# State-space scan over chunks of eight steps, with the first raw activations read back ahead of the residual

## The chip, the cores and the metric

One core of a Trainium2 chip runs the whole program. The metric is device time in microseconds (us), the median over several runs; the profile is of one execution. TensorE multiplies matrices, VectorE, ScalarE and GpSimd (POOL in the profile) work on elements, SyncE (SP) does nothing but issue DMAs.

## What is computed

A two-block transformer over 256 tokens of width 1024, in fp32. The first block runs sliding-window attention and a state-space layer side by side, adds both to the input, and then a retrieval layer (8 heads pick 16 of 16384 single-neuron experts each). A second block has two attention layers. The part that matters here is the state-space layer, over 272 positions (16 meta tokens and 256 tokens): 32 groups of 16 channels, each of which drives 64 complex states.

```python
def s5_ssm(u, a_re, a_im, log_dt, b_re, b_im, c_re, c_im, d, glu_w, glu_b):
    ...
    _, _, s_r, s_i = lax.associative_scan(_complex_linear_combine, (a_r, a_i, bu_r, bu_i), axis=1)
    y = (jnp.einsum('blgn,gpn->blgp', s_r, c_re.astype(jnp.float32))
         - jnp.einsum('blgn,gpn->blgp', s_i, c_im.astype(jnp.float32))
         + d.astype(jnp.float32).reshape(SSM_GROUPS, SSM_CH) * uf)
    z = jax.nn.gelu(y.reshape(B, L, SSM_WIDTH), approximate=False)
    z = z * jax.nn.sigmoid(z @ glu_w.astype(jnp.float32) + glu_b.astype(jnp.float32))
```

Before it, a fixed complex factor abar and a map bbar are made of the parameters, and bu is bbar times the input of a step: s(t) = abar s(t-1) + bu(t), y(t) = Re(c s(t)) + d u(t).

## The kernel before

`body` (line 1583) runs four stages: `first_half` (line 176: the first attention and the state-space layer), `peer` (line 725: the retrieval layer), `even` and `odd` (the second block). A framework records all instructions, works out their dependencies and puts each engine's instructions in an order by the times that it expects; at run time each engine, and SP's queue of DMAs, goes through its own list in order. `c.after(b, a)` fixes that b is put behind a.

Weights come in half tiles of 128x1024 fp32 through `Feed` (line 63): SP loads them (line 88) into five buffers, ScalarE rounds each to H (line 100), and VectorE or GpSimd subtracts to get the rest Lo (line 102); a product of matrices is then three passes, H by H, H by Lo and Lo by H (`mm3`, lines 1643 to 1645). SP can load into a buffer only when Lo of its last contents is done.

In `first_half` the input is normalised and turned (`turn(k)`, lines 227 to 233, of which hH and hL, lines 232 and 233, are the two halves), and u is projected from it into four accumulators (`up`). Then a background of three generators, `kv`, `q` and `attention`, is interleaved by hand with the state-space layer: `f.run` (line 439) draws a step from `ssm_scan` and lets the background spend the number of ns that the step yields. The output projection of the attention half (`out_part`, added to h at line 356) ends the background; the state-space half's own `out_part` ends the stage.

The state-space layer goes by 8 groups of two pairs of channel groups, step by step in time. `ssm_setup` (line 449) makes tables tabc and tabs of the cosine and sine of the state's angle for 137 steps, by doubling (lines 547 to 559). `ssm_scan` (line 563) maps u to the states on TensorE (line 590), turns them by the tables so that the recurrence becomes real (`turn`, lines 597 on GpSimd and 599 on VectorE, sums at lines 628 and 629), scans in two halves of 136 steps on VectorE (line 637, joined at lines 641 to 645), turns back, and maps the states to the outputs on TensorE (line 614). The d term, Gelu, the GLU's matmuls (line 658) and `ssm_glu` follow. At line 262 ScalarE's queue fills wscr, 8 MB in DRAM, with zeros.

In `peer`, a first expert phase multiplies the normed input with 16384 columns and stores the raw activations of two blocks at a time in DRAM (ascr<-ga, line 792). Meanwhile GpSimd scatters the picked weights into wscr, one indirect DMA a slot (`scatter`, line 997, DMA at line 1002), and then fetches them (line 804). The second expert phase reads the raw activations back (`back`, line 818, DMA at line 820), multiplies them by the weights (line 845), splits them (lines 847 and 848) and multiplies with the second expert matrix (line 835). Before its first matmul `refill` (line 1697) allocates c.x, which takes the place of xH, and loads the residual (line 1702) and the parameters of the second block (line 1704). In the recorded code the first two reads stand before `refill`, but their order on SP is the framework's.

Of the kernel before, what the change touches and what calls it, by code (L numbers as in the profile page):

```python
# [19 lines left out]
FT = mybir.dt.float32  # L20
# [31 lines left out]
NPKA = _cols(PKA, [("are", 16), ("aim", 16), ("ldt", 16), ("n1g", 8), ("pow", 8)])  # L52
NPK1 = _cols(PK1, [("bre", 256), ("bim", 256), ("cre", 256), ("cim", 256), ("d", 4), ("glub", 4), ("ag", 4), ("sg", 4),
# [119 lines left out]
HL = L // 2  # L173


def first_half(c):
# [4 lines left out]
    with ExitStack() as ctx:  # L181
# [26 lines left out]
        tab = ssm_setup(c, one, inp, P1)  # L208
        S5 = next(tab)
# [5 lines left out]
        uT = one.tile([128, 4, L], FT, name="uT")  # L215
        nc.scalar.activation(uT.rearrange("p a b -> p (a b)")[:16, :D], mt, AF.Square, accum_out=ss[:16, 2:3])
# [6 lines left out]
        hH = inp.tile([128, 8, L], FR, name="hH")  # L223
        hL = inp.tile([128, 8, L], FR, name="hL")
# [14 lines left out]
        next(tab, None)  # L239
        for q in range(4):  # L240
            H, Lo = c.feed.take()
            for k2 in range(2):
                k = 2 * q + k2
                for ct in range(4):
                    s = slice(k2 * 512 + ct * 128, k2 * 512 + (ct + 1) * 128)
                    c.mm3(up[ct][:, :L], H[:, s], Lo[:, s], hH[:, k], hL[:, k], k == 0, k == 7)
                if k + 3 < 8:
                    turn(k + 3)
                if k + 3 == 7:
                    for _ in range(4):  # L250
                        next(tab, None)
        uH = one.tile([128, 4, L], FR, name="uH")
        uL = one.tile([128, 4, L], FR, name="uL")
        for ct in range(4):
            nc.scalar.copy(uH[:, ct], up[ct][:, :L])
            c.usplit = V.tensor_sub(uL[:, ct], up[ct][:, :L], uH[:, ct].bitcast(FT))
            nc.scalar.copy(uT[:, ct], up[ct][:, :L])
        for _ in tab:
            pass
        S5[-1]()  # L260
# [176 lines left out]
        zT = one.tile([128, 4, T], FT, name="zT")  # L437
        f.spend(8000)
        f.run(ssm_scan(c, f, one, P1, uH, uL, uT, S5, zT, lambda: glu, res))
        work = ctx.enter_context(tc.tile_pool(name="b1g", bufs=1, side="right", reuse_waits="tile"))  # L440
        zH, zL, zr = ssm_glu(c, work, P1, zT, res["glu"])
# [4 lines left out]
def ssm_setup(c, one, tmp, P1):  # L446

    nc, tc = c.nc, c.tc
    V, G = nc.vector, nc.gpsimd
    small = lambda n, w=16: one.tile([128, w], FT, name=n)  # L450

    dt, ar, th, mag = small("dt"), small("ar"), small("th"), small("mag")
    nc.scalar.activation(dt, P1("ldt"), AF.Exp)
    V.tensor_tensor(th, P1("aim"), dt, op=OP.mult)
    V.tensor_tensor(ar, P1("are"), dt, op=OP.mult)
    nc.scalar.activation(mag, ar, AF.Exp)

    flat = lambda t: t.rearrange("p n j -> p (n j)")
    ang, kk, s2 = (tmp.tile([128, 8, 16], FT, name="pw%d" % i) for i in range(3))
    s1, pc = (one.tile([128, 8, 16], FT, name="pw%d" % i) for i in range(3, 5))  # L460
    V.tensor_tensor(ang, th[:, None, :].to_broadcast([128, 8, 16]), P1("pow")[:, :, None].to_broadcast([128, 8, 16]), op=OP.mult)
    ang, kk, s1, s2, pcf = (flat(t) for t in (ang, kk, s1, s2, pc))
    V.tensor_scalar(kk, ang, 1.0 / (2 * math.pi), MAGIC_ROUND, op0=OP.mult, op1=OP.add)
    V.tensor_scalar(kk, kk, MAGIC_ROUND, None, op0=OP.subtract)
    V.scalar_tensor_tensor(ang, kk, -TWO_PI_HI, ang, op0=OP.mult, op1=OP.add)
    V.scalar_tensor_tensor(ang, kk, -TWO_PI_LO, ang, op0=OP.mult, op1=OP.add)
    V.tensor_scalar(ang, ang, 3.1415925, -3.1415925, op0=OP.min, op1=OP.max)
    nc.scalar.activation(s1, ang, AF.Sin)
    nc.scalar.activation(s2, ang, AF.Sin, scale=0.5)
    tabc = one.tile([128, 16, HL + 1], FT, name="tabc")  # L470
    tabs = one.tile([128, 16, HL + 1], FT, name="tabs")
    bT = [one.tile([128, 2, 4, 128], FR, name="bT%d" % i) for i in range(2)]
    cd = [one.tile([128, 16, 2, 16], FT, name="cd%d" % i) for i in range(3)]
    bd = [tmp.tile([128, 16, 2, 16], FT, name="bd%d" % i) for i in range(2)]
    for t in bd + cd:
        G.memset(t, 0.0)
    V.memset(tabc[:, :, 0:1], 1.0)
    V.memset(tabs[:, :, 0:1], 0.0)
    V.tensor_tensor(s2, s2, s2, op=OP.mult)
    V.tensor_scalar(pcf, s2, -2.0, 1.0, op0=OP.mult, op1=OP.add)  # L480
    ps = s1.rearrange("p (n j) -> p n j", n=8)
    C1, S1 = pc[:, 0], ps[:, 0]
    yield tabc, tabs, mag, bT, cd, lambda: maps_T()


    nr, ni, den, t0, t1, cr, ci = (small("c%d" % i) for i in range(7))
    c.after(V.tensor_tensor(nr, mag, C1, op=OP.mult), c.normed)
    V.tensor_scalar(nr, nr, -1.0, None, op0=OP.add)
    c.after(V.tensor_tensor(ni, mag, S1, op=OP.mult), c.normed)
    V.tensor_tensor(den, P1("are"), P1("are"), op=OP.mult)  # L490
    V.tensor_tensor(t0, P1("aim"), P1("aim"), op=OP.mult)
    V.tensor_tensor(den, den, t0, op=OP.add)
    V.reciprocal(den, den)
    V.tensor_tensor(t0, nr, P1("are"), op=OP.mult)
    V.tensor_tensor(t1, ni, P1("aim"), op=OP.mult)
    V.tensor_tensor(cr, t0, t1, op=OP.add)
    V.tensor_tensor(cr, cr, den, op=OP.mult)
    V.tensor_tensor(t0, ni, P1("are"), op=OP.mult)
    V.tensor_tensor(t1, nr, P1("aim"), op=OP.mult)
    V.tensor_tensor(ci, t0, t1, op=OP.subtract)  # L500
    V.tensor_tensor(ci, ci, den, op=OP.mult)
    yield

    def maps():

        bre, bim = (P1(n).rearrange("p (j q) -> p j q", j=16) for n in ("bre", "bim"))
        m = [tmp.tile([128, 16, 16], FT, name="m%d" % i) for i in range(4)]
        crb, cib = cr[:, :, None].to_broadcast([128, 16, 16]), ci[:, :, None].to_broadcast([128, 16, 16])
        G.tensor_tensor(m[0], bre, crb, op=OP.mult)
        G.tensor_tensor(m[1], bim, cib, op=OP.mult)  # L510
        G.tensor_tensor(m[2], bim, crb, op=OP.mult)
        G.tensor_tensor(m[3], bre, cib, op=OP.mult)
        for g in range(2):
            s = slice(g * 64, g * 64 + 64)
            V.tensor_tensor(bd[0][s, :, g], m[0][s], m[1][s], op=OP.subtract)
            V.tensor_tensor(bd[1][s, :, g], m[2][s], m[3][s], op=OP.add)

    def maps_T():
        cre, cim = (P1(n).rearrange("p (j q) -> p j q", j=16) for n in ("cre", "cim"))
        for z in range(2):  # L520
            p = c.psum("m")
            for i in range(4):
                nc.tensor.transpose(p[:, i * 128:(i + 1) * 128], bd[z][:, 4 * i:4 * i + 4], c.ident)
# [1307 lines left out]
```

## Time and profile before

| | us |
|---|---|
| median of 3 runs | 1405.28 (1401.46, 1405.28, 1407.55) |
| the profiled execution | 1401.81, of which the span is 1400.0 |
| TensorE busy | 1299.6 (93% of the span) |
| VectorE busy | 991.6 (71%) |
| ScalarE busy | 655.1 (47%) |
| GpSimd busy | 527.2 (38%) |
| granted TensorE clock, mean | 0.95 |

The span is the time from the first to the last instruction of the profiled execution. Busy times of engines overlap. A matmul in fp32 leaves two records in the trace, one of fp32r or a transpose leaves one; records of TensorE overlap in its pipeline, so its pace is read from the starts of neighbours or from a row of several. PEclk is the clock that TensorE was granted, as a share of 2.4 GHz.

### The profile page before, as it was taken

What the parts mean: (1) busy time and instruction counts of PE and PEld (TensorE: products, weight loads), DVE (VectorE), ACT (ScalarE), POOL (GpSimd) and SP (SyncE); (2) the same over time, 40 slices, a digit from 0 to 9 for tenths busy, and PEclk for the clock granted to TensorE, in tenths of its full rate; (3) what the DMA queues carried; (4) which work ended last, traced back from release to release, by engine and by line L of the source; (5) the groups of instructions that cost most, each with busy time, mean ns of one, the idle gap of its engine ahead of it and who ended that gap; (6) DMA issues with size and microseconds to landing.
All of it is one profiled execution on the core that took longest, in us unless ns stands there. A gap on an engine that the chain in (4) does not pass through costs nothing.

```text
span 1400.0 us, 21202 instructions
## 1 busy us (share of the span) xinstructions
PE 1299.6 (93%) x7744; PEld 1107.8 (79%) x7744; DVE 991.6 (71%) x2229; ACT 655.1 (47%) x1138; POOL 527.2 (38%) x282
## 2 busy tenths in 40 slices
PE   5677888999999999999799999999998989979998
PEld 4554568999999999999678788888866768766777
DVE  8898957888988766664688855555557765585734
ACT  5323335545445445444444445444454545533552
POOL 4664642188787878600000000000024327441243
PEclk9865898999999999999899999999999999997999
DMA  6820036588888777896899966655664335551231
GB/s 222 287 61 31 16 100 217 163 226 222 224 226 228 190 205 203 256 371 216 281 308 314 308 195 188 188 190 187 193 212 151 90 106 166 198 157 55 82 106 60
DMA packets 103912, 259.01 MB, mean 185 GB/s; under 512 B 27120, under 2 KB 35696, under 8 KB 102528
## 3 DMA queue, kind: packets, MB, share of 16 engines
q1 hardware_dynamic: 65728, 224.04, 49.6%
q10 hardware_dynamic: 17472, 25.17, 5.1%
q0 software_dynamic: 20608, 8.46, 5.0%
q8 instruction: 60, 0.98, 0.3%
q14 instruction: 44, 0.36, 0.1%
HBM read 230.04 MB, written 27.33 MB: 184 GB/s over the span
## 4 chain that ended last, share of the span: by engine, by line
PE 71%; DVE 19%; DMA 5%; issue 3%; POOL 1%; ACT 1%; SPq 0%; DVEq 0%; POOLq 0%; ACTq 0%
PE ps L835 18%; PE ps L1643 10%; PE ps L1644 10%; PE ps L1645 10%; PE pr L1643 4%; PE pr L1645 4%; PE pr L1644 4%; DMA ga<-ascr 4%; DVE Lo L102 3%; PE m L1235 2%; PE ps L1043 2%; PE o L1280 1%; DVE sg L637 1%; DVE rs L1660 1%; POOL pr L597 1%
## 5 line engine op out<-in xcount | busy, mean ns | idle before, releaser
L101 ACT CAST H<-w 128x1024 fp32r<-128x1024 f32 (+1 forms) x370 | 386.5, 1046 | 511.5 <-PE ps L835 182.3
L102 DVE TENSOR_TENSOR Lo<-w,H 128x1024 fp32r<-128x1024 f32 x290 | 364.3, 1257 | 165.9 <-ACT H L101 165.7
L102 POOL TENSOR_TENSOR Lo<-w,H 128x1024 fp32r<-128x1024 f32 (+1 forms) x80 | 193.8, 2427 | 718.8 <-ACT H L101 704.8
L1643 PE MATMUL ps<-xH,H 128*128 128x256 f32 x1024 | 290.8, 284 | 0.0
L835 PE MATMUL ps<-H,a 128*128 128x512 f32 x1024 | 281.3, 396 | 8.0 <-ACT a L847 7.6
L1644 PE MATMUL ps<-xL,H 128*128 128x256 f32 x1024 | 287.8, 281 | 0.0
L1645 PE MATMUL ps<-xH,Lo 128*128 128x256 f32 x1024 | 287.6, 281 | 0.0
L1002 POOL DMA_INDIRECT wscr<-sent x128 | 243.5, 1903 | 72.5 <-issue 37.8
L835 PEld LDWEIGHTS ps<-H,a 128*128 128x128 f32 x1024 | 193.6, 189 | 54.0 <-ACT a L847 7.8
L1643 PEld LDWEIGHTS ps<-xH,H 128*128 128x128 f32 x1024 | 193.1, 189 | 0.0
L1644 PEld LDWEIGHTS ps<-xL,H 128*128 128x128 f32 x1024 | 193.1, 189 | 0.0
L1645 PEld LDWEIGHTS ps<-xH,Lo 128*128 128x128 f32 x1024 | 192.9, 188 | 0.0
L835 PE MATMUL ps<-Lo,a 128*128 128x512 f32 x512 | 161.7, 397 | 0.6 <-DVE Lo L102 0.6
L835 PEld LDWEIGHTS ps<-Lo,a 128*128 128x128 f32 x512 | 96.8, 189 | 24.3 <-DVE Lo L102 1.8
L845 DVE TENSOR_TENSOR act<-ga,act 128x256 f32<-128x256 f32 x128 | 47.3, 420 | 26.8 <-DMA ga<-ascr 26.5
L1643 PE MATMUL pr<-H,exH 128*128 128x512 f32 x128 | 54.5, 427 | 0.9 <-ACT exH L1083 0.9
L847 ACT CAST a<-act 128x256 fp32r<-128x256 f32 x128 | 51.4, 402 | 6.8 <-DVE act L845 6.8
L1643 PE MATMUL pr<-H,oxH 128*128 128x512 f32 (+1 forms) x128 | 52.8, 415 | 1.1 <-ACT oxH L1083 1.1
L848 DVE TENSOR_TENSOR a<-act,a 128x256 fp32r<-128x256 f32 x128 | 53.5, 419 | 0.0
L1644 PE MATMUL pr<-Lo,exH 128*128 128x512 f32 x128 | 53.0, 414 | 0.0
L1645 PE MATMUL pr<-H,oxL 128*128 128x512 f32 (+1 forms) x128 | 52.6, 411 | 0.0
L1030 DVE TENSOR_TENSOR o<-cstt,sel 128x512 f32<-128x512 f32 x32 | 22.1, 692 | 43.0 <-PE ps L1043 43.0
(471 smaller groups left out, 2164.4 us busy)
## 6 DMA issues: line engine op xcount, KB each, us to landing
w<-in_ut SPq DMA_DIRECT2D x128, 512.0 KB
w<-in_pv SPq DMA_DIRECT2D x128, 512.0 KB
ascr<-ga ACTq DMA_DIRECT2D x64, 256.0 KB
ga<-ascr SPq DMA_DIRECT2D x64, 256.0 KB
w<-in_we SPq DMA_DIRECT2D x32, 512.0 KB
w<-in_wod SPq DMA_DIRECT2D x28, 512.0 KB
wscr<-zero ACTq DMA_DIRECT2D x4, 2048.0 KB
w<-in_wqy SPq DMA_DIRECT2D x16, 512.0 KB
```

The costliest lines, as they stand in the source:

```text
L101: self.last = self.nc.scalar.copy(H, self.loaded[u])
L102: eng.tensor_sub(Lo, self.loaded[u], H.bitcast(FT))
L835: nc.tensor.matmul(acc[2 * th + n], a[:, s], b[:, n * 512:(n + 1) * 512], start=first and e == 0, stop=last and e == 2)
L845: V.tensor_tensor(src, ga[:, blk % 2], src, op=OP.mult)
L847: copied = nc.scalar.copy(aH, src)
L848: V.tensor_sub(aL, src, aH.bitcast(FT))
L1002: ins = c.nc.gpsimd.indirect_dma_start(out=c.wscr.rearrange("i b (t o) -> (i b t) o", o=1), out_offset=bass.IndirectOffsetOnAxis(ap=t.bitc ...
L1043: nc.tensor.matmul(p[:, a * 128:(a + 1) * 128], o1[:, a], o2[:, a], start=True, stop=True)
L1235: nc.tensor.matmul(sp[:, :off + nk], q(h)[:, ts], k(h)[:, :off + nk], start=True, stop=True)
L1643: nc.tensor.matmul(o, ah, bh, start=first, stop=False)
L1644: nc.tensor.matmul(o, ah, bl, start=False, stop=False)
L1645: nc.tensor.matmul(o, al, bh, start=False, stop=last)
```

## The change

Instead of a step, the state-space layer now goes by a chunk of 8 steps: 272 positions are 34 chunks. Of each chunk, a matrix W maps its 8x16 inputs to its contribution to the state; a scan over 34 chunks carries the state (one table R of 34 angles); a matrix T maps the 8x16 inputs to the 8x16 outputs inside the chunk (from the impulse response K, which holds d too), and a matrix G maps the state at the chunk's start to its outputs. All four maps are fp32 matmuls. To have a chunk's 8x16 inputs on 128 partitions, u goes through DRAM (udr) and comes back as U in 8 DMAs; K goes through DRAM (kdr) and comes back as T in 16; the outputs z go through DRAM (zdr) in 16 DMAs and come back in 4. All of these are on SP's queue. GpSimd's rotations, the split copies uH and uL and the copy uT go.

```diff
+        if q == 0:
+            ssm.coefficients()
+        ssm.enter(up)
+        ssm.maps()
...
+    def coefficients(self):
...
+        shape = [128, 16, SJ, 16]
+        cut = lambda t: t[:, :16 * SJ * 16].rearrange("p (j m q) -> p j m q", j=16, m=SJ)
+        self.W = [self.temp("W", z) for z in range(2)]
+        t = [self.temp("tw", 2 + z) for z in range(2)]
+        self.product(cut(self.W[0]), cut(self.W[1]), [A[:, z, :, :SJ, None].to_broadcast(shape) for z in range(2)],
+                     [bb[z][:, :, None, :].to_broadcast(shape) for z in range(2)], [cut(x) for x in t])
+    def enter(self, up):
...
+        for ct in range(4):
+            nc.scalar.copy(uP[:, ct].rearrange("p j c -> p c j"), up[ct][:, :L].rearrange("p (c j) -> p c j", j=SJ))
+            nc.sync.dma_start(c.udr[ct * 128:(ct + 1) * 128], uP[:, ct])
+        src = c.udr.rearrange("(g q) j c -> q j g c", q=16)
+        for j in range(SJ):
+            m = SJ - 1 - j
+            nc.sync.dma_start(U[16 * m:16 * m + 16], src[:, j])
+    def response(self):
...
+        nc.sync.dma_start(c.kdr.rearrange("(a p) n -> p a n", p=128), K.rearrange("p a m q -> p a (m q)"))
+        self.T = [one.tile([128, 16, 128], FT, tag="WT", name="T", bufs=2) for z in range(2)]
+        src = c.kdr.rearrange("(g q) n -> q g n", q=16)
+        for h in range(2):
+            for j in range(SJ):
+                m = SJ - 1 - j
+                nc.sync.dma_start(self.T[h][16 * m:16 * m + 16], src[:, 16 * h:16 * h + 16, 16 * m:16 * m + 128])
+    def run(self, glu, out):
...
+                for j in range(j0, j0 + n):
+                    nc.tensor.matmul(p[:, (j - j0) * 2 * SC:(j - j0 + 1) * 2 * SC], self.WT[z][:, j],
+                                     self.U[:, 2 * j:2 * j + 2].rearrange("p g c -> p (g c)"), start=True, stop=True)
...
+        for z in range(2):
+            V.tensor_tensor_scan(flat(sc[:, z]), flat(self.mags), flat(m1[:, z]), 0.0, op0=OP.mult, op1=OP.add)
+        yield 2000
+        self.response()
...
+            if ct % 2:
+                h = slice(8 * ct - 8, 8 * ct + 8)
+                for i in range(SJ):
+                    nc.sync.dma_start(dst[:, i, h], zc[16 * i:16 * i + 16, h])
+                for k in (ct - 1, ct):
+                    nc.sync.dma_start(self.zT[:, k], c.zdr[k * 128:(k + 1) * 128].rearrange("p i c -> p (i c)"))
```

`maps` transposes W (32 transposes into the slots WT, which T takes over later) and makes R by doubling, six levels of six operations; `outputs` makes G, six operations of 128x2304. In `run` the outputs of four channel tiles take 8 matmuls by T (32 columns) and 8 by G (64 columns) each.

The second part fixes the order in which the second expert phase begins: pk2, and then the residual, are put behind the read-back of the second pair of blocks. The third makes scatters wait for the scatters of the head before, and the fetch of wscr for the last ones.

```diff
-            nc.sync.dma_start(ga, c.ascr[blk // AB][:, blk % AB:blk % AB + 2])
+            backs.append(nc.sync.dma_start(ga, c.ascr[blk // AB][:, blk % AB:blk % AB + 2]))
...
-        refill()
+        refill(backs[1])
...
-            nc.sync.dma_start(c.x, hscr)
-            nc.sync.dma_start(pk2, A["pk2"])
+            for m in (nc.sync.dma_start(pk2, A["pk2"]), nc.sync.dma_start(c.x, hscr)):
+                after(m, behind)
...
-                    nc.gpsimd.dma_start(act[:, b, 128:], c.wscr[:, b])
+                    pk.wait(nc.gpsimd.dma_start(act[:, b, 128:], c.wscr[:, b]).ins, pk.last)
...
+        self.wait(ins, self.before)
```

## Rows read from the trace of the kernel before

**Rows 1.** Windows view: stretch, length, busy us of each engine, granted clock, DMA share.
```profile
0.00:18.00 18.00, 2.53 (x9) 1.66 (x9) 14.56 (x54) 9.97 (x17) 8.05 (x13) 1.00 0.77 288
18.00:38.00 20.00, 17.74 (x117) 16.50 (x118) 18.84 (x44) 9.17 (x16) 9.31 (x8) 1.00 0.56 175
38.00:60.00 22.00, 12.44 (x82) 10.29 (x80) 21.69 (x35) 8.81 (x18) 16.58 (x10) 0.87 1.00 340
60.00:150.00 90.00, 73.93 (x300) 45.71 (x301) 78.90 (x144) 31.92 (x84) 51.48 (x27) 0.65 0.16 54
150.00:208.00 58.00, 49.19 (x253) 35.47 (x252) 43.78 (x88) 18.93 (x34) 30.26 (x15) 0.97 0.20 57
250.00:660.00 410.00, 408.77 (x3471) 408.40 (x3471) 310.79 (x737) 202.28 (x309) 257.92 (x138) 1.00 0.81 230
```

**Rows 2.** Groups of VectorE, 0 to 208 us.
```profile
L637 DVE TENSOR_TENSOR_SCAN sg<-mags,pr 128x272 f32<-128x272 f32 x32 | 24.7, 797 | 0.0
L599 DVE TENSOR_TENSOR pr<-tabc,sg 128x1088 f32<-128x1088 f32 x8 | 15.1, 1893 | 0.1
L548 DVE TENSOR_TENSOR w<-tabc,pw 128x512 f32<-128x512 f32 (+6 forms) x18 | 15.1, 862 | 0.0
L599 DVE TENSOR_TENSOR pr<-tabc,bu 128x1088 f32<-128x1088 f32 x8 | 13.8, 1722 | 4.3 <-ACT bu L591 4.3
L629 DVE TENSOR_TENSOR pr<-pr 128x544 f32<-128x544 f32 x8 | 9.9, 1241 | 0.0
L628 DVE TENSOR_TENSOR pr<-pr 128x544 f32<-128x544 f32 x8 | 7.7, 968 | 2.5 <-POOL pr L597 2.5
```

**Rows 3.** Groups of GpSimd, 0 to 208 us.
```profile
L597 POOL TENSOR_TENSOR pr<-tabs,bu 128x544 f32<-128x544 f32 x16 | 31.0, 1963 | 7.9 <-ACT bu L591 7.9
```

**Rows 4.** Timeline of VectorE, first layer: start, us, instruction.
```profile
2.42 0.18 DVE L490 TENSOR_TENSOR c<-pka 128x16 f32<-128x16 f32 x1 [1.46 <-DMA pka<-in_pka]
...
37.57 0.69 DVE L559 TENSOR_TENSOR tabs<-w,w 128x512 f32<-128x512 f32 x1
...
107.37 0.72 DVE L637 TENSOR_TENSOR_SCAN sg<-mags,pr 128x272 f32<-128x272 f32 x1
...
111.02 1.28 DVE L599 TENSOR_TENSOR pr<-tabc,sg 128x1088 f32<-128x1088 f32 x1
...
141.15 2.42 DVE L599 TENSOR_TENSOR pr<-tabc,sg 128x1088 f32<-128x1088 f32 x1
...
206.12 1.40 DVE L356 SCALAR_TENSOR_TENSOR h<-m,zh,h 128x512 f32<-128x512 f32 x2
```

**Rows 5.** Timeline of TensorE, first layer.
```profile
157.89 1.33 PE L416 MATMUL o<-vr,PT 128*128 128x64 f32 x10
...
185.28 2.03 PE L614 MATMUL y<-pr,cd 128*32 128x272 f32 x16
...
188.33 1.99 PE L658 MATMUL b<-zT,glu 128*128 128x256 f32 x8 [1.03 <-ACT zT L656]
```

**Rows 6.** Timeline of SP's DMA issues, start of the kernel.
```profile
0.74 0.39 SPq L187 DMA_DIRECT2D pka<-in_pka  x1
```

**Rows 7.** DMA view, 279 to 350 us: packets, MB, share of 16 engines.
```profile
q0 software_dynamic: 4454, 0.02, 15.2%
```

**Rows 8.** DMA view, 30 to 70 us.
```profile
q10 hardware_dynamic: 8256, 8.39, 64.8%
```

**Rows 9.** Timeline of SP's DMA issues around 666 us.
```profile
666.11 0.33 SPq L1702 DMA_DIRECT2D x<-hscr  x1
666.49 6.38 SPq L820 DMA_DIRECT2D ga<-ascr  x2
```

**Rows 10.** Timeline of TensorE around 670 us.
```profile
673.71 1.22 PE L835 MATMUL ps<-H,a 128*128 128x512 f32 x2 [7.63 <-ACT a L847]
```

**Rows 11.** Timeline of GpSimd, scatters into wscr.
```profile
354.61 1.73 POOL L1002 DMA_INDIRECT wscr<-sent  x1 [3.87 <-DMA wscr<-sent]
```

**Rows 12.** Waits of SP's queue, 0 to 208 us: total, times, longest.
```profile
SPq L88 <- POOL Lo L102: 156.0, 17, 53.2
```

More of the change, by code (lines that the diff above doesn't have):

```diff
@@ L652, in ssm_scan @@
-    yield "exps"
-    acc = [c.psum("b") for _ in range(2)]
-    def mix(k):
-        nc.scalar.activation(zT[:, k], zT[:, k], AF.Gelu)
-        for co in range(4):
-            m = nc.tensor.matmul(acc[co // 2][:, co % 2 * T:co % 2 * T + T], glu()[:, k * 512 + co * 128:k * 512 + (co + 1) * 128], zT[:, k],
-                                 start=(k == 0 and co % 2 == 0), stop=(k == 3), skip_group_check=True)
-            if k == 0:
-                if co % 2:
-                    c.after(m, first)
-                first = m
-        return m
@@ new lines, in run @@
+            yield 1500
+        self.outputs()
+        flat = lambda t: t.rearrange("p j c -> p (j c)")
+        both = lambda z: self.R[:, None, z].to_broadcast([128, 2, 16, SC])
+        room = lambda n, i: self.temp(n, i)[:, :2 * 16 * SC].rearrange("p (z j c) -> p z j c", z=2, j=16)
+        m1, m2 = room("m1", 1), room("m2", 2)
+        V.tensor_tensor(m1, st, both(0), op=OP.mult)
+        V.tensor_tensor(m2, st, both(1), op=OP.mult)
+        V.tensor_tensor(m1[:, 0], m1[:, 0], m2[:, 1], op=OP.add)
@@ new lines, in run @@
+        V.tensor_tensor(m1[:, 1], m1[:, 1], m2[:, 0], op=OP.subtract)
+        yield 3000
+        sc = room("sc", 3)
+        for z in range(2):
+            V.tensor_tensor_scan(flat(sc[:, z]), flat(self.mags), flat(m1[:, z]), 0.0, op0=OP.mult, op1=OP.add)
+        yield 2000
+        self.response()
+        m1, m2 = room("m1", 0), room("m2", 1)
+        V.tensor_tensor(m1, sc, both(0), op=OP.mult)
+        V.tensor_tensor(m2, sc, both(1), op=OP.mult)
+        t = self.temp("S", 2)
+        S = [t[:, 1024 * z:1024 * z + 1024].rearrange("p (j g c) -> p j g c", j=16, g=2) for z in range(2)]
@@ new lines, in run @@
+        for z in range(2):
+            nc.gpsimd.memset(S[z], 0.0)
+            for g in range(2):
+                r = slice(64 * g, 64 * g + 64)
+                V.tensor_tensor(S[z][r, :, g], m1[r, z, :, 1:SC - 1], m2[r, 1 - z, :, 1:SC - 1], op=(OP.subtract, OP.add)[z])
+        yield 3000
+        zc = self.temp("zc", 3)[:, :32 * (SC - 2)].rearrange("p (g c) -> p g c", g=32)
+        self.zT = self.temp("zT", 0)[:, :4 * T].rearrange("p (a t) -> p a t", a=4)
+        n = SC - 2
+        dst = c.zdr.rearrange("(g p) i c -> p i g c", p=16)
@@ new lines, in run @@
+        yield "exps"
+        acc = [c.psum("b") for _ in range(2)]
+        yield 8000
+        for k in range(4):
+            for co in range(4):
+                m = nc.tensor.matmul(acc[co // 2][:, co % 2 * T:co % 2 * T + T], glu()[:, k * 512 + co * 128:k * 512 + (co + 1) * 128], self.zT[:, k],
+                                     start=(k == 0 and co % 2 == 0), stop=(k == 3), skip_group_check=True)
+                if k == 0:
+                    if co % 2:
+                        c.after(m, first)
+                    first = m
+            yield 500
@@ L676, in ssm_glu @@
+        out["glu"] = acc
+        yield 1e9
 def ssm_glu(c, work, P1, zT, glu):
@@ L995, in send, with wait @@
             self.sends.pop(0)()
+    def wait(self, ins, those):
+        for b in those:
+            self.c.tc.add_manual_dep(ins, b.name, mybir.DependencyInfo(mybir.DependencyClass.Sync, mybir.DependencyReason.DATA), reason="adds")
     def scatter(self, i):
```

395 lines of the change are left out of this document (178 added, 217 removed).

## The prediction

> **What bounds the kernel now.** I read the windows view first. From 250 to 660 us TensorE is busy 408.77 of 410 us at a granted clock of 1.00: nothing off TensorE that ends there earlier can shorten that stretch, and whatever the first layer saves moves it forward whole. The first layer, up to 208 us, is another matter. Between 60 and 150 us VectorE is busy 78.90 of 90 us while TensorE is granted 0.65, a mix of its two levels, 1.2 and 2.4 GHz [rows 1]. Weighted by the granted clock, TensorE's work there is only 2.5 + 17.7 + 12.44 x 0.87 + 73.93 x 0.65 + 49.19 x 0.97 = 127 us at full clock, against 207.5 us that the layer takes: its last residual add starts at 206.12 us and ends 1.40 us later [rows 4].
>
> The groups of VectorE say whose work this is. Scan, rotations, their sums and the table products, six groups, take 24.7 + 15.1 + 15.1 + 13.8 + 9.9 + 7.7 = 86 us [rows 2]; with some smaller ones of the same functions I put the state-space share at about 120 us. GpSimd helps the rotations, 31.0 us for the forward ones alone [rows 3], and this seems to cost VectorE time: one rotation of 128x1088 took 1.28 us once and 2.42 us another time [rows 4]. So the first layer is a chain on VectorE, and TensorE waits for it at a low clock. That is the stage the change rewrites.
>
> **VectorE, part by part.** Removed: the 120 us above. Added, by 1.28 us for 1088 elements and 0.69 us for 512, a slope of 1.02 ns an element [rows 4]:
> - The product W (six operations of 2048): 6 x 2.26 = 13.6 us. The product G (six of 2304): 6 x 2.52 = 15.1 us.
> - Powers of A, coefficients and bbar, some 40 operations of 16 to 256 elements: I put them at 9 us. The rotation table R, 36 such operations: 8 us.
> - Rotation of 1088 elements twice and two halves: 2 x 1.28 + 2 x 0.71 = 4 us (0.71 by the 0.69 row); two scans of 544, each at twice the 0.72 us of 272 elements: 2.9 us; the way back, 2 x 1.28 + 4 x 0.69 = 5.3 us.
>
> That is some 58 us, so VectorE sheds about 60 us. The upper end is 2.42 in place of 1.28 for every large product, 26 us more; I take the low one, because GpSimd loses the rotations and keeps only the weight splits and two memsets.
>
> **TensorE.** Removed: 128 records of the output maps at 2.03 / 16 = 0.127 us [rows 5], 16 us; 96 of the input maps at the same pace, 12 us. Added in fp32, two records a matmul (the transposes, one each, at the same pace): 32 transposes, 64 records for the states, 64 for the response, 128 for the outputs, 288 in all. Their moving sides have 32 to 128 columns. The nearest row is 64 columns against a 128x128 weight: 1.33 us for 10, some 0.12 us in steady flow [rows 5]. 288 x 0.12 = 35 us, so 7 us more than before: TensorE then has 134 us of work at full clock. With no useful work in the first 16 us, about 150 us is the floor of the layer.
>
> **The new chain.** u is ready at 38 us now. W's products stand ahead of the last three splits of the input in the order of the code, so I add 5 us: 43. Then:
> - The eviction and write of u to DRAM, 4 us: a small DMA landed 1.7 us after its issue (0.74 to 2.42) [rows 4, 6]. Eight reads of rows of 136 B: 512 packets each, 4096 in all. A 4-byte packet took 15.2% x 16 x 71 / 4454 = 39 ns of an engine [rows 7], a 1 KB one 64.8% x 16 x 40 / 8256 = 50 ns [rows 8], so size hardly counts and 4096 packets on 16 engines are 10 to 13 us. The zero fill keeps the engines full until past 60 us [rows 1], so I double it: U lands at about 70.
> - States: 64 x 0.12 = 7.7 us and evictions, 79. Rotation, scan and way back, 12 us: 91. G and the response fit beside this.
> - T: its slots are those of the transposed W, free at 79; 16 issues at 0.39 us [rows 6] and 4096 packets of 512 B, 13 us. T lands near 96, a little after the states. Outputs 15.4 us, with some 14 us of attention and output projection between them: 125.
> - z by DRAM, last pair: 8 issues, 2048 packets and two landings, 13 us: 138. Last GLU matmuls, 4 us: 142.
> - From the last GLU matmul, ended at 190.3 (188.33 + 1.99) [rows 5], to 207.5 now lie 17 us: 159.
>
> The chain says 159, the floor of TensorE 150; both share engines, and clock drops like the present one come on top. I take 166: **41 us saved**. The ends: 150 (58 us saved), and 190 (17 us), with TensorE still at half clock for half of its work.
>
> The skill speaks against the detour. The Trainium skill, "DMA: Bandwidth & Descriptors", Specifications, asks for at least 512 B a transfer for line rate, with a read-modify-write below that; U's and z's rows are shorter. The 39 ns row, which adds into DRAM, does not show such a penalty. If it doubled those packets, the chain would be some 18 us longer by estimate, and the whole would come to 1376; by the 39 ns row it stays 1358.
>
> **The read-back.** The first matmuls of the second expert phase start at 673.71 us, after 7.63 us of idle time, and run at half pace [rows 10]. SP issues the 1 MB x<-hscr at 666.11 and the two ga behind it from 666.49 over 6.38 us [rows 9]. With ga first, at worst the first ga is issued at 666.2, lands by the 1.7 us of a small load plus some for its 256 KB, and 4.4 us of the gap go. At best its slot is free earlier, and the gap goes with the slow start behind it, 10 us. I take 6 us, near the lower end, because the second ga still waits for the last store of its buffer. x is first added after the whole phase, pk2 is read eight blocks in; their 1.4 MB are covered by the loaded weights, and without this cover cost the same 4 us again.
>
> **Scatter waits.** Each head's scatters now wait for all sixteen before. One such wait stands in the trace already, 3.87 us [rows 11]. Five more are 19 us on GpSimd, which does nothing else then; the fetch of wscr behind them would end so much later, but its first piece is needed only at the second expert phase and the others over the following 350 us. Nothing, unless that fetch runs past the phase's start; then a few us.
>
> **Sum.** The profiled execution took 1401.81 us, span 1400.0. 1401.8 - 41 - 6 = 1354.8. The median shown is 1405.28, 3.5 higher, so on the scale of the medians 1358. The three runs lie 0.43% apart: within 0.5% is no change that can be told.
>
> **Rivals.**
> - *More than forecast*: work from the background fills all three DRAM trips, and VectorE has room for it: TensorE's floor binds, 150 us. For it: VectorE falls to some 118 us of work. Against it: every trip ends in a wait of TensorE's own queue. 1405 - 58 - 8 = 1339. Chance 0.17.
> - *TensorE stays slow*: idle gaps at the trips keep the granted clock near the present 0.65 [rows 1] for much of the layer; end at 188. For it: 60 to 150 us now shows just this. 1405 - 19 - 5 = 1381. Packets of U and z at 80 to 100 ns in place of 39 to 50 would end near there too (18 us on the chain, 1376), and their chance is counted here; against them stands the 4-byte row [rows 7]. Chance 0.23.
> - *Slower: SP's queue holds everything*. The change puts 49 DMAs on SP, which issues in order. Its weight loads waited 156.0 us for GpSimd's splits, once 53.2 us at a stretch [rows 12]. A trip's DMA behind such a load waits for the background to use weights, and the output projection's weights wait behind T and z. All in series: 43 + 27 (U) + 15 + 16 + 14 (states, VectorE, response at half clock) + 24 (T) + 31 (outputs) + 14 (z) + 8 (GLU) + 24 (one output projection at half clock) + 17 = 233. Then 1405 + 25 - 6 = 1424. It decides once SP stands still for some 50 us more than I allow. Against it: the order of SP follows the program's planned times. Chance 0.07.
> - *No gain*: half of that, or the trips cost the 41 us and only the read-back stays: about 1400. Chance 0.05. That the change does less than it says is here too: if ga's slot frees only at 666.5, its part shrinks to 4 us.
>
> My forecast keeps 0.48. Faster by more than 0.5% (below 1398) are forecast, first and second rival: 0.88; same 0.05; slower 0.07. The range runs from 1337, the best case, to 1392, which takes in the slow-TensorE case with its upper end, and leaves out about 2 in 10.
>
> **What would show it.** Right: in the windows of the first layer VectorE's busy time falls from 178 to about 118 us [rows 1], the layer's last residual add ends near 166 us, granted clock above 0.8 between 60 and 150; U's DMAs land near 70, T's near 96. The gap before the first matmul of the second expert phase shrinks from 7.63 us to below 3.5. Everything from 250 to 660 us keeps its length. Wrong: long waits of SP's own queue ahead of U, T or z, or TensorE waiting over 15 us at one of them; or VectorE still above 90% busy.

## The result: slower by 0.85%, and the profile after

The changed kernel takes 1415.74 us in the median of five runs (1413.33 to 1418.00), the kernel before 1402.05 us in five runs beside it: a ratio of 1.0085, 95% interval 1.0061 to 1.0109. The forecast was 1358 us, range 1337 to 1392. The profiled execution took 1414.31 us, its span 1412.3.

The windows view of the changed kernel, for the stretches of [rows 1]:

```profile
18.00:38.00 20.00, 13.55 (x80) 12.14 (x79) 18.03 (x21) 7.32 (x13) 5.79 (x2) 0.95 0.26 80
38.00:60.00 22.00, 12.17 (x83) 11.93 (x84) 22.00 (x37) 5.75 (x10) 4.67 (x1) 0.66 0.48 159
60.00:150.00 90.00, 59.88 (x359) 47.09 (x358) 43.81 (x105) 30.82 (x82) 16.25 (x8) 0.73 0.62 150
150.00:208.00 58.00, 48.99 (x215) 43.04 (x216) 7.83 (x26) 11.08 (x19) 9.54 (x4) 0.71 0.30 62
```

VectorE lost the work it was to lose: 107 us from 0 to 208 us instead of 178, and between 150 and 208 us it does 7.83 us in 58. Yet the layer got longer. Its last residual adds, in the timeline of VectorE, which ended at 207.5 us before [rows 4]:

```profile
223.00 1.40 DVE L347 SCALAR_TENSOR_TENSOR h<-m,zh,h 128x512 f32<-128x512 f32 x2
```

They end at 224.4, **16.9 us later** (some of the expectations below take 223.8). At the second expert phase 4.6 us come back: TensorE's wait in front of it is 3.02 us instead of 7.63 [rows 10]:

```profile
684.74 1.22 PE L865 MATMUL ps<-H,a 128*128 128x512 f32 x2 [3.02 <-ACT a L877]
```

16.9 - 4.6 = 12.3 us, and the spans differ by 12.3; that it fits to the tenth is luck, as the phase's first matmul comes 11.0 us later than before (684.74 against 673.71). So the question is what the first layer does with a VectorE that has so much less to do. Three waits of TensorE tell it, in its timeline, each with the time that it sat idle before:

```profile
47.83 0.28 PE L228 MATMUL m<-cstt,mt 16*128 16x16 f32 x1 [14.97 <-DVE hL L233]
...
78.91 0.76 PE L1678 MATMUL p<-H,hH 128*128 128x512 f32 x1 [12.25 <-DVE ks L288]
...
115.55 1.94 PE L330 MATMUL m<-cstt,xs 128*128 128x128 f32 x8 [14.77 <-DVE xs L323]
```

They are 42 us, all for VectorE: for the last splits of the input, for the key norm and for the query norm. During the first and the third VectorE was busy with the new work. During the second it was not, but for the end of G's last product (66.9 us). Its timeline around the three:

```profile
34.07 2.28 DVE L449 TENSOR_TENSOR W<-A,bb 128x2048 f32<-128x2048 f32 x1
...
45.08 2.28 DVE L454 TENSOR_TENSOR W<-W,tw 128x2048 f32<-128x2048 f32 x1
47.29 0.90 DVE L233 SCALAR_TENSOR_TENSOR hL<-m,pka,hH 128x272 fp32r<-128x272 f32 x2
...
70.67 0.88 DVE L284 TENSOR_REDUCE kss<-ks 128x2 f32<-128x128 f32 x3 [3.73 <-ACT ks L283]
...
72.00 2.27 DVE L1689 TENSOR_SCALAR ri<-rs 128x6 int32<-128x6 int32 x1
...
104.27 1.28 DVE L644 TENSOR_TENSOR_SCAN sc<-mags,m 128x544 f32<-128x544 f32 x1
...
113.15 0.69 DVE L657 TENSOR_TENSOR S<-m,m 64x512 f32<-64x512 f32 x1
114.71 1.29 DVE L323 TENSOR_TENSOR xs<-p,rs 128x512 f32<-128x512 f32 x2
```

W's six products run ahead of the last splits (34.07 to 47.3), rotation and scan ahead of the query norm. In the second wait VectorE stood idle 3.73 us for ScalarE's squares of the keys, in front of which ScalarE evicted transposed W (67.50) and rounded weights (68.46); and two of the key norm's 128x6 operations took 2.27 and 2.26 us beside a weight split on GpSimd (69.59 to 76.53), where their neighbours take 0.17. The query norm ends at 116.0 us, as it did before the change, where its row reads:

```profile
114.65 1.27 DVE L332 TENSOR_TENSOR xs<-p,rs 128x512 f32<-128x512 f32 x2
```

Attention therefore starts no earlier than it did, and what before ran beside it, the state-space outputs, now stands behind it. SP's issues and TensorE's outputs show that part:

```profile
54.29 2.06 SPq L542 DMA_DIRECT2D udr<-uP  x4
...
61.95 11.19 SPq L546 DMA_DIRECT2D U<-udr  x8
...
131.17 0.38 SPq L607 DMA_DIRECT2D kdr<-K  x1
134.05 12.30 SPq L613 DMA_DIRECT2D T<-kdr  x16
```

K leaves only at 131 us, as its 32 matmuls stand between the attention's scores (126.6 us), and T's trip keeps the 16 DMA engines busy until about 155. The output matmuls run at 164.86 to 188.4, behind the attention's output projection. z's trip follows with only the first half of the GLU's matmuls beside it (TensorE waits 3.71 and 3.83 us for it), and the last GLU matmuls start at 201.75. From the timeline of TensorE, two groups of the outputs early and two late, and one window:

```profile
167.49 0.58 PE L670 MATMUL y<-U,T 128*128 128x32 f32 x4
167.91 0.64 PE L677 MATMUL y<-S,G 128*128 128x64 f32 x4
...
171.29 1.01 PE L670 MATMUL b<-U,T 128*128 128x32 f32 x4
172.11 1.09 PE L677 MATMUL b<-S,G 128*128 128x64 f32 x4
```

```profile
170.00:175.00 5.00, 5.00 (x25) 5.00 (x25) 0.00 (x0) 0.05 (x1) 0.00 (x0) 0.50 0.00 0
```

Until 168.8 a group of four takes 0.37 to 0.47 us (the distance of the starts), then 0.79 to 0.89: the granted clock falls to 0.50, 1.2 GHz, while TensorE is busy without a gap.

### The profile page after: what moved, and what is told of

It is laid out like the page before. It is cut to its first block, busy times and chain, and to the rows that moved or that the text cites. A ratio compares the mean times of both kernels' runs of the same rounds, so it can differ in the third digit from the quotient of the medians.

```text
span 1412.3 us, 21249 instructions
## 1 busy us (share of the span) xinstructions
PE 1293.4 (92%) x7800; PEld 1123.5 (80%) x7800; DVE 935.5 (66%) x2151; ACT 647.7 (46%) x1119; POOL 457.5 (32%) x237
## 4 chain that ended last, share of the span: by engine, by line
PE 76%; DVE 16%; DMA 4%; issue 2%; ACT 2%; SPq 0%; DVEq 0%; ACTq 0%
PE ps L865 21%; PE ps L1678 9%; PE ps L1679 9%; PE ps L1680 9%; PE pr L1678 4%; PE pr L1680 4%; PE pr L1679 4%; DMA ga<-ascr 3%; PE m L1270 2%; PE ps L1078 2%; DVE Lo L102 2%; PE o L1315 1%; DVE rs L1695 1%; DVE rs L1696 1%; PE p L1678 1%
## 5 line engine op out<-in xcount | busy, mean ns | idle before, releaser
L1036 POOL DMA_INDIRECT wscr<-sent x128 | 239.6, 1872 | 87.8 <-issue 36.8
L1680 PE MATMUL pr<-H,exL 128*128 128x512 f32 x128 | 52.7, 412 | 0.0
```

Of the source, the lines that this page charges most:

```text
L1036: ins = c.nc.gpsimd.indirect_dma_start(out=c.wscr.rearrange("i b (t o) -> (i b t) o", o=1), out_offset=bass.IndirectOffsetOnAxis(ap=t.bitc ...
L1680: nc.tensor.matmul(o, al, bh, start=False, stop=last)
```

## The experiments

The theory after this reading: the loss is one of order. VectorE and TensorE take their work in a row that keeps the attention's chain where it was and puts the new chain behind it. The rival: the new work itself is too slow (trips through DRAM, narrow matmuls), whatever its order. Ratios are to the kernel before, run beside them on the same chip (1402.7 us in the first group, 1404.44 in the second, 1402.97 and 1402.73 in the last two).

### One order at a time

**u_first**: W's products, and the four multiplications of G, behind the last split.

```
-            if q == 0:
-                ssm.coefficients()          # with W's products in it
+        ssm.weights()                       # W's products, behind the loop
+        for op in ops: c.after(op, c.split) # the same for G's
```

> Edit: the six products of W and the first four of G carry an order edge behind the last split of the input (the last hL), so VectorE finishes the splits first. Theory (the time was lost in the order of VectorE's work): in the changed kernel TensorE waits 14.97 us for hL while VectorE runs the W products; here that wait goes, u is ready at 38 to 41 us instead of 54.5, the states end some 10 us earlier than 97.2, and the first layer ends 6 to 13 us earlier than 223.8: 1402 to 1409 us. Rival (the trips through DRAM set the end): K still leaves at 131 us, because its matmuls stand between the attention scores, T still lands near 157 and the end moves by under 3 us: 1412 to 1416 us.

Measured: 1414.51 us, 1.0084 (1.0065 to 1.0104). The rival's number, and in part its reason: K still left at 130.49 us and T was issued at 133.37. But what u had gained was lost well before that. TensorE's waits, in its timeline:

```profile
46.28 1.97 PE L564 MATMUL m<-cstt,W 128*128 128x128 f32 x8 [6.68 <-DVE W L457]
...
78.85 0.76 PE L1686 MATMUL p<-H,hH 128*128 128x512 f32 x1 [19.94 <-DVE ks L289]
114.87 1.94 PE L331 MATMUL m<-cstt,xs 128*128 128x128 f32 x8 [14.76 <-DVE xs L324]
```

u was written out from 36.09 us on instead of 54.29, 18 us earlier, and at 78.85 all of it was gone: TensorE now waits 19.94 us for the key norm, which stands behind G's products on VectorE (58.81 to 75.3 us; three of them took 4.23, 4.69 and 4.69 us beside GpSimd's weight splits instead of 2.55). The next place in the row took the gain.

**resp_early**: G's products and the response ahead of the states.

```
         yield 8000
+        self.outputs()
+        self.response()
...
-        self.response()                     # behind the scan
```

> Edit: the G products and the response matmuls stand ahead of the states matmuls instead of behind the scan, nothing else. Theory (order): K is done near 82 us instead of 130.6, the loads of T follow the end of the states (97) instead of 134 and land by 125 instead of 157; half of the output matmuls then run while attention waits for its exponentials, and some 8 to 12 of the 23.5 us that the outputs took behind the attention's output projection are saved: 1402 to 1408 us. Rival (TensorE's half clock and its one row of work set the end, whenever T lands): the outputs cost the same wherever they stand and push attention back by as much, 1413 to 1417 us.

Measured: 1409.99 us, 1.0046 (1.0033 to 1.0059), about 5.5 us better than the changed kernel; between the two. K left at 77.69 and T was issued at 97.00 instead of 134.05, and half of the outputs ran ahead of the attention's PV matmuls. But in the window from 120 to 140 us the granted clock (third number from the end) is 0.50, with TensorE busy 18.35 of 20 us:

```profile
120.00:140.00 20.00, 18.35 (x62) 13.70 (x62) 7.71 (x38) 11.55 (x40) 0.00 (x0) 0.50 0.13 50
```

And key and query norm come no earlier: TensorE's first matmuls behind them start at 78.88 and 116.17 us, against 78.91 and 115.55.

**outs_first**: besides, the attention's output projection behind the last output matmul.

```
+                    c.outs = nc.tensor.matmul(y[...], self.G[z][...], S[z][...])
...
+                for m in ms: after(m, c.outs)      # the projection's matmuls
```

> Edit: as in resp_early, and the attention's output projection (48 matmuls of 512 columns, some 14 us) stands behind the last output matmul, so that the trip of z through DRAM (13.2 us, 188.6 to 201.75 in the changed kernel) has work beside it. Theory: about 10 of those 13 us are hidden, and the first layer ends some 10 us earlier than with resp_early: 1397 to 1403 us. Rival (the projection only waits in turn, and its own tail of VectorE work comes at the end): 1408 to 1414 us.

Measured: 1404.96 us, 1.0013 (0.9997 to 1.0029), another 4.6 us. TensorE no longer waits for z at all. In resp_early it had waited 3.67 and 3.21 us for it, so most of that wait was gained; the projection and its residual adds now come late instead.

### The read-back by itself

**readback_alone**, on the kernel before:

```
-        refill()
+        refill(backs[1])                    # the second ga
...
-            nc.sync.dma_start(c.x, hscr)
-            nc.sync.dma_start(pk2, A["pk2"])
+            for m in (nc.sync.dma_start(pk2, A["pk2"]), nc.sync.dma_start(c.x, hscr)):
+                after(m, behind)
```

> Edit: the kernel before with only the new order of the reads (first raw activations, then constants, then residual); the state-space part and the scatters as before. Theory: the second expert phase starts about 5 us earlier, as its transition shrank in the changed kernel by 223.8-207.5 less 684.7-673.7 = 5.3 us: 1395 to 1399 us against 1402. Rival: the gain there came from another shift in the queue and the order is worth nothing: 1401 to 1403 us.

Measured: 1397.11 us, 0.9966 (0.9946 to 0.9985), 4.8 us faster. TensorE's wait there:

```profile
667.53 1.22 PE L836 MATMUL ps<-H,a 128*128 128x512 f32 x2 [3.01 <-ACT a L848]
```

**readback_undone**: the same lines turned back in the changed kernel.

> Edit: the changed kernel with the old order of the reads (residual, constants, then raw activations). Theory: the 5 us come back as a loss, 1419 to 1422 us, and the state-space part with the scatter waits alone is then 1.2 to 1.4% slower than the kernel before. Rival: no change, 1415 to 1417 us.

Measured: 1418.59 us, 1.0117 (1.0097 to 1.0137), so 4.5 us lost; the same price from both sides. What is then left of the change is 1.17% of 1402.7, 16.4 us, and the first layer alone is 16.9 us longer. That leaves nothing for the scatters' added waits, give or take 3 us by the intervals. The trace says why: GpSimd waited for scatters 8 times, 29 us in all (before 3 times, 12 us), but its last fetch of wscr is issued at 613.44 us, some 70 us before the second expert phase needs it.

### Why the outputs run at half clock

**wide_outs**:

```
-  m = nc.tensor.matmul(y[:, o * n:(o + 1) * n], self.T[...], self.U[:, 2 * j + g, 2:], ...)
+  m = nc.tensor.matmul(y[:, :8 * n], self.T[...], self.U[:, 8 * ct:8 * ct + 8, 2:], ...)
```

> Edit: each of the 32 matmuls by T takes 256 columns of U (eight groups) instead of 32, all added up in the same bank, so that the outputs of this part are sums of what doesn't belong together; order and count stay. In the changed kernel these and the 64-column matmuls by G between them fall from 0.108 to 0.21 us per record after 4 us, at a granted clock of 0.50, while TensorE has no gap. Theory (it is the width: TensorE is held back when it moves few columns, busy or not): the granted clock stays at 0.9 or more through this stretch, the G records stay near 0.11 us, and the stretch takes 15 to 18 us instead of 23.5 although it moves more: 1408 to 1411 us. Rival (the clock fell for what came before, or for the type of the operands): clock 0.50 as before, records by T near 0.25 us, the stretch takes 24 us or more: 1415 to 1419 us.

Measured: 1412.30 us, 1.0061 (1.0041 to 1.0081), some 3 us better than the changed kernel by the medians, with intervals that overlap; what the run shows is in its trace. The same window and two groups:

```profile
170.00:175.00 5.00, 5.00 (x32) 4.60 (x31) 0.00 (x0) 0.38 (x1) 0.00 (x0) 1.00 0.00 0
```

```profile
170.20 1.08 PE L670 MATMUL b<-U,T 128*128 128x256 f32 x4
171.12 0.55 PE L677 MATMUL b<-S,G 128*128 128x64 f32 x4
```

The granted clock stays at 1.00 from 160 to 185 us. A group by G, in which nothing was changed, takes 0.39 us to the next start (171.12 to 171.51) where it took 0.88. The stretch takes 21 us (165.02 to 186.1) instead of 23.5 with eight times the columns by T; my 15 to 18 left out what those columns cost, 0.92 us a group. So the columns that are moved decide it here, not the operands' type or an earlier gap.

### All orders together

**order_all**: W behind the splits, G behind the key norm, rotation and scan behind the query norm (with 7 us more of attention's work planned ahead of them), the response right behind the states, the output projection behind the output matmuls planned by then, which interleaves the two.

```
+        for op in ops: c.after(op, c.split)   # W
+        for op in g: c.after(op, c.kvn)       # G
+        self.response()                       # behind the states
+        yield 7000
+        c.after(op, c.qn)                     # first products of the rotation
+        after(m, c.outs)                      # output projection
```

> Edit, all of it order: the products of W behind the last split; the products of G behind the key norm's last multiply; the rotation and the scan behind the query norm; the response matmuls right behind the states; the attention's output projection behind the output matmuls that the program has issued by then. Theory (the loss is the order in which VectorE and TensorE take their work, and each place that a single edge frees is taken by the next): u ready at 38 to 41 us, key norm by 65 instead of 78.9, query norm by 95 instead of 114.7, T landed by 125, the trip of z partly beside the output projection, the first layer ends at 190 to 205 us instead of 223.8: 1382 to 1397 us. Rival (the work itself is more than what it replaces: output matmuls at half clock, three trips through DRAM one behind the other): the end stays above 212 us, over 1403 us.

Measured: **1376.90 us, 0.9797 (0.9770 to 0.9824)**, faster than both kernels: 2.0% than before, 2.9% than the changed one. Not an operation was taken out or made faster. Of the 2.0%, the read-back gives 0.34% by itself; whether the kernel before would also gain from another order was not tried. Windows, query norm and last residual adds:

```profile
60.00:150.00 90.00, 73.24 (x458) 59.96 (x458) 54.29 (x118) 34.37 (x89) 25.62 (x10) 0.79 0.54 108
150.00:186.00 36.00, 29.72 (x139) 23.70 (x139) 17.06 (x36) 11.64 (x19) 12.42 (x5) 0.95 0.35 93
```

```profile
96.26 1.29 DVE L324 TENSOR_TENSOR xs<-p,rs 128x512 f32<-128x512 f32 x2
...
183.78 1.40 DVE L348 SCALAR_TENSOR_TENSOR h<-m,zh,h 128x512 f32<-128x512 f32 x2
```

The query norm is done at 97.5 instead of 116.0, the layer at 185.2 instead of 224.4. TensorE's granted clock from 120 to 140 us, where narrow output matmuls now stand among the 512-column ones of the projection, is 1.00. It falls to 0.55 from 142.5 to 146 us, behind eight narrow groups in a row (139.44 to 143.03).

### What each order is worth

Each of the next leaves one out of order_all, whose ratio is 0.9797; differences of ratios are turned into us with 1402.7.

**all_but_u**:

```
-        ssm.weights()                       # W's products back into coefficients()
-        for op in ops: c.after(op, c.split)
```

> Edit: order_all (1376.9 us) with the products of W back where the change has them, ahead of the last three splits; its other edges stay. Theory (the orders add up, each worth what stands behind it): TensorE waits some 15 us for hL again, u is ready near 54 us, and as nothing behind it has slack the end moves back by 8 to 14 us: 1385 to 1391 us. Rival (u early alone gave 1 us, so it is worth as little here): 1376 to 1379 us.

Measured: 1383.54 us, 0.9861 (0.9836 to 0.9886), 0.64% or 9 us worse, with some 5 us of uncertainty either way. In the profiled executions the layer ends 3.4 us later than order_all's (at 188.57) and the span is 5.4 us longer, so the order is worth 3 to 9 us. u is written from 48.17 us on instead of 35.54, and TensorE waits 11.30 us for the last split. Alone, and with G's multiplications moved too, the same edge (one `c.after`) had given 0 to 1 us.

**all_but_outs**:

```
-                for m in ms: after(m, c.outs)
```

> Edit: order_all without the edges that hold the attention's output projection behind output matmuls, so that some of the output matmuls run behind it in one block. Theory (narrow matmuls in a block drop the clock to 0.50, among matmuls of 512 columns they keep 1.00; and z's trip loses its cover): the block costs some 5 us more and the trip of z up to 9 us more, 1385 to 1392 us. Rival (order within TensorE is worth nothing, as its work is the same): 1375 to 1380 us.

Measured: 1381.66 us, 0.9842 (0.9814 to 0.9870), 6 us worse, again within some 5 us, a little less than expected. The layer ends 5.6 us later, at 190.77. The second half of the outputs runs in one block (146.54 to 154.5), at whose end the granted clock falls (0.55 from 155 to 160 us), and the wait for z grows from 3.65 to 6.36 us:

```profile
167.00 6.74 PE L702 MATMUL b<-zT,glu 128*128 128x256 f32 x16 [6.36 <-DMA zT<-zdr]
```

**all_but_resp**:

```
-        self.response()                     # behind the states
+        self.response()                     # behind the scan
```

> Edit: order_all with the response matmuls back behind the scan. Theory: K is done near 115 to 124 instead of 90 us, as its matmuls then stand between the attention's PV matmuls, T lands near 150 instead of 125, and outputs, z and the end come 15 to 25 us later: 1392 to 1402 us. Rival (T's arrival has slack, the attention sets the end): 1376 to 1381 us.

Measured: 1400.84 us, 0.9981 (0.9961 to 1.0000), 26 us worse; the layer ends at 211.97. TensorE waits for T, with PV (131 us) and the transposes behind it (134.5) done, and then runs the outputs at half pace:

```profile
143.74 1.03 PE L679 MATMUL y<-U,T 128*128 128x32 f32 x4 [9.18 <-DMA T<-kdr]
144.59 1.09 PE L686 MATMUL y<-S,G 128*128 128x64 f32 x4
```

The 26 us are not the response's alone: the edge that is kept holds the attention's output projection behind these outputs, so it waits for T too. By itself, in resp_early, the same order gave 5.5 us.

**all_but_q**, and **q_room** with only the second of its two lines:

```
-        yield 7000
-        c.after(op, c.qn)
```

> Edit: order_all without the edge that holds the rotation and the scan behind the query norm (and without the room given for it). Theory: the scan's 14 us of VectorE work go ahead of the query norm again, the attention's scores begin some 8 to 12 us later, PV and the output projection with them; the outputs come earlier and fill part of it: 1380 to 1386 us. Rival (VectorE's total decides, not which goes first): within 3 us of order_all, 1374 to 1380 us.

Measured: 1403.06 us, 1.0002 (0.9990 to 1.0014), 29 us worse, far outside. The query norm moved by 9 us only:

```profile
105.25 1.29 DVE L324 TENSOR_TENSOR xs<-p,rs 128x512 f32<-128x512 f32 x2
```

But with the room for the norm the planner's place for the outputs went too: they ran in two blocks (135.6 to 146.1 and 158.3 to 171.9 us), all ahead of the projection and from 139.4 on at half clock. In one of them:

```profile
140.00:150.00 10.00, 10.00 (x49) 10.00 (x49) 0.00 (x0) 0.97 (x2) 0.00 (x0) 0.50 0.12 15
```

Two things in one run, so the next parts them.

> Edit: order_all without the edge that holds the rotation and the scan behind the query norm, but with the room for it kept, so that TensorE's order is that of order_all, matmul for matmul, and VectorE's alone changes. Theory (the 26 us that all_but_q lost are two things: the query norm is done 9 us later, at 106.5 instead of 97.5, and the outputs go in two blocks of 16 and 15 us, at half clock, ahead of the output projection): this run has the first alone and loses 6 to 10 us, 1383 to 1387 us. Rival (VectorE's order carries it all): 1398 to 1404 us.

Measured: 1387.47 us, 0.9882 (0.9859 to 0.9905), 12 us worse, near the theory. Of the 29 us, some 12 are VectorE's order and some 17 what the planner did with the outputs. TensorE's order here is the one of order_all, but scores and PV ran longer at half clock (0.57 from 120 to 140 us). The query norm starts at 105.99 and the layer ends 11.9 us after order_all's (195.66 + 1.40):

```profile
195.66 1.40 DVE L348 SCALAR_TENSOR_TENSOR h<-m,zh,h 128x512 f32<-128x512 f32 x2
```

The four parts, 9 + 6 + 26 + 29, come to 70 us, and all of them together are worth 40 (1.0085 to 0.9797). They don't add up. A reason, argued and not tested, is that the chains are in series at some points and side by side at others, and that an order which is kept can hold other work behind the one that is left out, as the projection in all_but_resp.

### GpSimd for half of G

**pool_g**:

```
-        V.tensor_tensor(self.G[0], ...)     # three of them, behind the key norm
+        nc.gpsimd.tensor_tensor(self.G[0], ...)   # behind the last split
```

> Edit: order_all with three of the six products of G (those of its real part) on GpSimd, behind the last split, while VectorE keeps the other three. Theory (with the order mended, VectorE's work between the key norm and the response sets when K leaves and when the query norm runs): the response matmuls come some 7 us earlier than 89.8 us, T lands 5 to 7 us earlier, the query norm 3 to 7 us, and the end 3 to 7 us: 1370 to 1374 us. Rival (T waits for its room, which the states free, or TensorE's own work from 100 us on sets the end; or GpSimd's long products hold back the splits of the weights): 1375 to 1383 us.

Measured: 1381.85 us, 0.9852 (0.9828 to 0.9877), 8 us worse, the rival's side. From the timelines of GpSimd, VectorE and TensorE:

```profile
31.82 4.13 POOL L589 TENSOR_TENSOR G<-pk,A 128x2304 f32<-128x2304 f32 x1
```

```profile
31.92 6.17 DVE L450 TENSOR_TENSOR W<-A,bb 128x2048 f32<-128x2048 f32 x1
```

```profile
75.76 0.76 PE L1689 MATMUL p<-H,hH 128*128 128x512 f32 x1 [14.74 <-DVE ks L289]
```

Beside GpSimd's product a W product took 6.17 us instead of 2.28, and the key norm, beside which GpSimd's later products and the splits delayed by them ran (57.45 to 73.6 us), kept TensorE waiting 14.74 us, where order_all waits 9.83. The layer ends 6.2 us later. This is the prediction's guess from [rows 4] (1.28 against 2.42), now with GpSimd's own row beside VectorE's. The Trainium skill, "GPSIMD Engine Reference", Architecture, says that GpSimd's physical SBUF ports are shared with VectorE; the two rows agree.

## Why the prediction was wrong, step by step

- *What bounds the kernel*: half right. Whatever the first layer gains or loses does come through nearly whole: order_all's layer ends 39.2 us before the changed kernel's (224.4), and its span is 36.5 us shorter. But "the first layer is a chain on VectorE" took a busy engine for a chain. What the layer waits for is a row, VectorE's above all. Of the 71 us that VectorE lost, 56 lay behind the query norm and only 15 ahead of it (102.6 to 87.9 us), and there it now stood idle for 27 us instead of 12. So the query norm didn't move (115.9 to 116.0): the new work stood ahead of what it waits for, on VectorE and on ScalarE.
- *VectorE, part by part*: right in size, 107 us instead of the 118 that I put.
- *The new chain*, the step that failed, at three places. First, W's products ahead of the last splits, for which I added 5 us: TensorE waited 14.97 us, and u came at 54.5 us instead of 43. All six products stood ahead, 13.2 us, and I had the six at 13.6 us in my own sum; 5 had no row behind it. Leaving the mended order out costs 3 to 9 us. U's trip itself was right, 26 us against 27, and only started late. Second, "G and the response fit beside this": nothing hides a matmul that is planned behind the scores. K left at 131 us, T landed near 155 instead of 96; this order is worth 26 us with the projection held behind the outputs, and 5.5 alone. Third, "some 14 us of attention and output projection between them": the attention was filler in my sum, though it has a chain of its own on the same engines: key norm, query projection, query norm, scores, PV. I never priced it. It sets the row of both kernels, and of order_all too, where the query norm at 97.5, not T (DMA at rest from 120 us, outputs from 126), starts the end.
- *TensorE*: 288 records at 0.12 us. In steady flow at full clock they take 0.11, but in a block of narrow ones 0.21: the outputs took 23.5 us instead of 15.4. My "clock drops come on top" had 7 us for all of it.
- *T's trip*: 4096 packets of 512 B in 13 us, from the 39 and 50 ns rows. The DMA view from 134 to 158 us of the changed kernel, the busy share in 40 slices of 0.6 us, then packets, MB and share of 16 engines:

```profile
DMA  0289999999999999999999999999999991000000
q1 hardware_dynamic: 4352, 2.10, 96.4%
```

24 us x 16 x 0.964 / 4352 = 85 ns a packet. The times of packets overlap, so the trip is shorter than their sum: some 21 us from the first issue (134.05) to 155, against 13 put. The Trainium skill, "DMA: Bandwidth & Descriptors", Specifications, has 512 B as enough for line rate. Here 512 B in 85 ns are 6 GB/s for an engine, where the zero fill's 1 KB in 50 ns [rows 8] are 20; the measurement decides. In order_all, where T's trip lies beside scores and PV, TensorE does not wait for it.
- *z by DRAM* (13 us) and *the tail* (17 us): 13.2 and 17 us, right.
- *The signs named*: VectorE's 107 us came; the clock above 0.8, T near 96 and the layer's end near 166 did not. The longest wait of TensorE was 14.97 us, just under the 15 named as a sign of being wrong, and for a split instead of a trip.
- *The read-back*: 6 us put, 4.5 to 4.8 measured, by the reason given; the wait fell below 3.5 us as named.
- *Scatter waits*: nothing, as put: 29 us of them, off the path.
- *The rivals*: "TensorE stays slow" named the clock (0.73 and 0.71 came), but gave it to the trips' gaps and stopped at 1381. "SP's queue holds everything" had the sign and not the cause. The trips in series were indeed its picture, but in series with attention through the engines' rows, not through SP. I had written against it that the order "follows the program's planned times", and it was just that plan which failed.

What stays open: the 19 us between order_all's layer (185.2) and my 166. Three waits of TensorE before the attention are for VectorE again:

```profile
45.73 1.97 PE L564 MATMUL m<-cstt,W 128*128 128x128 f32 x8 [6.65 <-DVE W L457]
...
68.06 0.77 PE L1687 MATMUL p<-H,hH 128*128 128x512 f32 x1 [9.83 <-DVE ks L289]
...
97.09 1.94 PE L331 MATMUL m<-cstt,xs 128*128 128x128 f32 x8 [5.76 <-DVE xs L324]
```

22 us in all, so they could cover it, but no run took them away; in pool_g the first two were longer (10.51 and 14.74 us) and the third the same. In the second VectorE itself stood idle, for ScalarE's squares. Another candidate is the clock of the stretch behind them. Neither was tested. VectorE's row, then the window:

```profile
60.60 0.86 DVE L285 TENSOR_REDUCE kss<-ks 128x2 f32<-128x128 f32 x3 [6.61 <-ACT ks L284]
```

```profile
100.00:120.00 20.00, 17.69 (x55) 11.46 (x55) 15.21 (x48) 10.10 (x38) 1.84 (x2) 0.53 1.19 141
```

## What to carry to other kernels

Before work on a busy engine is counted as saved, write down which instruction on that engine the next engine waits for, and what stands ahead of it after the change; the row decides, not the sum. Do the same for the engine that this instruction waits for in its turn; here ScalarE's row held the key norm too. When a change adds a second chain to a stage, price the chain that was there as well, and test orders together: here one edge alone gave nothing and the set gave 2.9%. A block of narrow matmuls is worth trying dealt out among wide ones: the clock stayed up that way in order_all from 120 to 140 us. It is no sure cure, as in all_but_resp groups among the projection's matmuls still ran at half clock (0.82 to 0.89 us a group, 154 to 159 us).

## What the runs showed of the hardware

- TensorE's granted clock fell to 0.50 while it was busy all of the time (170 to 175 us, 5.00 of 5.00), with moving sides of 32 and 64 columns; with 256 columns in half of those matmuls it stayed at 1.00. A group of four 64-column records took some 0.88 us at that clock, 0.47 just before it fell.
- A VectorE product of 128x2048 took 6.17 us beside a GpSimd product, 2.28 alone; a 128x6 operation 2.27 us beside a GpSimd weight split, 0.17 alone.
- A 512-byte packet from DRAM to 16 partitions took 85 ns of a DMA engine by its share of busy time, a 1 KB packet of the zero fill 50 ns.
